# One threshold update for two query tiles in a bitwise search for the 256th largest score

## The chip, the cores and the metric

The kernel runs on one core of a Trainium2 chip. Its time is the device time of one execution, in microseconds (us); lower is better. Three runs of the kernel before took 3038.46, 3047.42 and 3047.6 us, so the median is 3047.42 us.

## The reference

Two transformer blocks run one after the other on a sequence of 1024 tokens with 1024 features. The change touches only the sparse attention of the first block. A small indexer scores every key for every query, and a query attends to its 256 best keys:

```python
dots = einsum('bthd,bsd->bths', qib, k_idx) * IDX_DIM ** -0.5      # 8 index heads, 64 wide
score = einsum('bth,bths->bts', wb * IDX_HEADS ** -0.5, relu(dots))
score = where(causal, score, -inf)
_, idx = top_k(score, 256)                                          # per query
...                                                                 # softmax over the 256 keys, 8 heads
```

The rest of the first block is a gated spatial unit, an output projection, and a feed-forward layer (FFN) of width 4096. The second block (a recurrence, a state space layer and another FFN) stands behind it and is not touched.

## The kernel before, in words

Tokens are cut into 8 query tiles of 128 rows, tile by tile on the 128 partitions. Tile `tt` can see keys up to its own end, so its scores are a matrix `sel[tt]` of 128 rows and (tt+1)*128 columns. Tiles 0 and 1 have at most 256 keys and need no search. The sequence is worked in two halves: tiles 0 to 3 (half A), beside the projections of both halves, and tiles 4 to 7 (half B), beside the output projection and the first FFN of half A.

The work on one tile has three steps. `index_score` (lines 622 to 649) makes the scores: TensorE products, a relu on ScalarE (L638), weighted sums on VectorE (L641, L643), and a causal fill on GpSimd (L648). `topk` (lines 651 to 698) finds, for each row, the value that 256 scores reach, one bit of its float pattern at a time. One bit is one step of three instructions on VectorE, each needing the one before: a count of the scores at or above the trial value (L669, over the whole row), a comparison of the count with 256 (L679, one element per partition) and the new trial value by bit operations (L680, one element per partition, two tensor inputs). There are 31 such steps per tile. Then the mask is written over the scores, ties included (L690 to L697). `attend` (lines 700 to 779) goes through the tiles in order, four pairs of heads each: TensorE products (L733, L734), mask and row maximum (L735), exponentials on ScalarE (L743), scaling (L746), transposes, a split in two parts (L760, L761), products with the values (L764), and sums into `ybT` (L770). The sums of squares of a finished tile (L778) feed `mix_in` (L803 to L818), which scales the attention result by L808 and L813 for the output projection `token_out`.

What sets the order of instructions on an engine is a scheduler with priorities and a model of times; each engine then runs its list in that order. The searches and everything marked `urgent` have the highest priority. Steps of two tiles whose code is in one call or in two are woven into one another wherever the scheduler finds both ready. Other projections and the FFN share VectorE with the searches: they empty TensorE's accumulators there (L302, L902) and split operands. GpSimd meanwhile makes the low parts of weights (L118) and sums for a modulation (L437).

In half A the calls are a search of tile 2 and one of tile 3. In half B they are one for tiles 4 and 5, one for 6, one for 7.

Of the kernel before, what the change touches and what calls it, by code (L numbers as in the profile page):

```python
# [8 lines left out]
F32 = mybir.dt.float32  # L9
F32R = mybir.dt.float32r  # L10
I32 = mybir.dt.int32
# [3 lines left out]
OP = mybir.AluOpType  # L15
# [6 lines left out]
HALF = 512  # L22
P = 128
# [11 lines left out]
class Kernel:  # L35
# [614 lines left out]

    def topk(self, tts):

        steps = [self.topk_steps(tt) for tt in tts if tt > 1]
        for _ in zip_longest(*steps):
            pass

    def topk_steps(self, tt):


        V = self.nc.vector  # L660
        n = (tt + 1) * P
        sel = self.sel[tt]
        junk = self.junk if tt > 3 else self.junk[:, tt % 2 * HALF:tt % 2 * HALF + HALF]

        def count(value, op):

            c = self.tinyS.tile([P, 4], I32, name=f"topk{tt % 2}")
            cnt = c[:, 0:1].bitcast(F32)
            V.tensor_scalar(junk[:, :n], sel, value, 0.0, op0=op, op1=OP.add, accum_out=cnt)  # L669
            return cnt, c[:, 1:2], c[:, 2:3]  # L670

        cnt, t, u = count(0.0, OP.is_ge)
        V.tensor_scalar(t, cnt, 256.0, 1.0, op0=OP.is_ge, op1=OP.subtract)
        V.tensor_scalar(u, t, 1 << 30, None, op0=OP.bitwise_xor)
        yield
        for b in range(30, -1, -1):
            t = u
            cnt, keep, u = count(t.bitcast(F32), OP.is_ge)
            V.tensor_scalar(keep, cnt, 256.0, float(1 << b), op0=OP.is_ge, op1=OP.mult)  # L679
            V.scalar_tensor_tensor(u, t, (1 << b) ^ (1 << b >> 1), keep, op0=OP.bitwise_xor, op1=OP.bitwise_xor)  # L680
            yield
        thr = u.bitcast(F32)
        before = count(thr, OP.is_gt)[0]
        ties = junk.bitcast(F16)
        k = ties.shape[1] // 2
        for c0 in range(0, n, k):
            w = min(k, n - c0)
            x = sel[:, c0:c0 + w]
            e, r = ties[:, :w], ties[:, k:k + w]
            V.tensor_scalar(e, x, thr, None, op0=OP.is_equal)  # L690
            V.tensor_tensor_scan(r, e, e, before, op0=OP.add, op1=OP.max)
            if c0 + w < n:
                before = self.tinyS.tile([P, 4], F32, name=f"topk{tt % 2}")[:, 0:1]
                V.tensor_copy(before, r[:, w - 1:w])
            V.scalar_tensor_tensor(r, r, 256.0, e, op0=OP.is_le, op1=OP.mult)
            V.scalar_tensor_tensor(x, x, thr, r, op0=OP.is_gt, op1=OP.add)
        V.tensor_scalar(sel, sel, -1.0, -MASKED, op0=OP.add, op1=OP.mult)  # L697
        yield

    def attend(self, tts, ybT, depth=1, through=True):  # L700

# [255 lines left out]
    def run(self):  # L957
        nc, I, tc = self.nc, self.I, self.tc
        with ExitStack() as at:
# [8 lines left out]
            with ExitStack() as sa:  # L968
                sg = self.pool("sgup", st=sa, side="right")
                self.ropep = self.pool("ropep", st=sa, side="right")  # L970
                self.score = self.pool("scoreA", st=sa, side="right")
                with ExitStack() as st:
                    tmp = self.pool("early", st=st)
                    self.cols_setup(tmp)
                    self.rope_setup(tmp)
                    self.cols_mod(tmp)
                    rows = [self.rowp.tile([P, D], F32, name="row") for j in range(3)]
                    rows.append(self.acc.tile([P, D], F32, name="acc"))
                    self.raws = self.pool("raws", 8, st=st)
                    sums = self.tp.tile([P, 512], F32, name="tp")  # L980

                    gains = lambda k0, k1: self.gain_part(k0, k1, sums)
                    biases = lambda k0, k1: self.ada_part(0, k0, k1, sums)
                    gains(0, PARTS[1])
                    rows = self.scaled_rows(rows, lambda t: I["x"][0, t * P:(t + 1) * P, :], scalar=True)
                    first = biases(0, PARTS[1])
                    next(first)
                    gen = self.norm_T(rows, self.s1, self.sh1, ("tp", "tp"), 3, PARTS[1:])
                    next(gen)
                    next(first, None)  # L990
                    hA = next(gen)

                    def parts():
                        for k0 in range(0, 8, 2):
                            if k0 and k0 in PARTS:
                                k1 = min([k for k in PARTS if k > k0] + [8])
                                gains(k0, k1)
                                for _ in biases(k0, k1):
                                    pass
                                next(gen)  # L1000
                            yield

                    self.wi = self.consts.tile([P, 8, 8], F32, name="wi")
                    self.sel = {}
                    self.ssx = {}
                    self.ssb = [self.consts.tile([P, 4], F32, name=f"ssb{i}") for i in range(2)]
                    self.proj(0, hA, "kvq", parts())
                    self.proj(0, hA, "qkw")

                    self.kT = self.k16.tile([P, 4, S], F32R, name="k16")  # L1010
                    self.kiT = self.kT[:, :, HALF:].rearrange("p (a b) t -> p a b t", a=2)
                    self.ki_stack(range(4))
                    for tt in (2, 3, 0, 1):
                        self.index_score(tt)
                self.ybp = long("ybp", 4)
                self.pT = long("pT", 2)
                self.proj(0, hA, "q")
                self.sgu_setup(sg)
                self.cols_rest()
                with ExitStack() as st:  # L1020
                    self.adac = self.pool("adac", 2, st=st)
                    self.pp = self.pool("ppA", 6, st=st)
                    self.vhl = [self.vp.tile([P, 4, 2, P], F32R, name="vhl0")]
                    p0 = tc.cur_priority
                    self.kv_stack(range(4))
                    ybA = [self.ybp.tile([P, HALF], F32, name="ybT") for k in range(4)]
                    with self.urgent():
                        self.topk((2,))
                        self.topk((3,))
                    with tc.high_priority(tc.cur_priority - p0):  # L1030
                        self.attend(range(4), ybA, 2)
                    self.proj(0, hA, "u")
                    rows = [self.rowp.tile([P, D], F32, name="row") for j in range(3)]
                    rows.append(self.adac.tile([P, D], F32, name="adac"))
                    rows = self.scaled_rows(rows, lambda t: I["x"][0, (4 + t) * P:(5 + t) * P, :])
                    hB = self.norm_T(rows, self.s1, self.sh1)
                    next(hB)
                    self.proj(0, hA, "v")
                    next(self.sgu_steps)
                    hB = next(hB)  # L1040
                    self.background = self.ada_rest()
                    for b in ("qkw", "kvq", "q", "u", "v"):
                        if b == "u":
                            mA = self.mix_gated(0)
                        self.proj(1, hB, b)
                        if b in ("qkw", "v"):
                            next(self.sgu_steps)
                    next(self.sgu_steps)
                    for _ in self.background:
                        pass  # L1050
                    self.ki_stack(range(4, 8))
                    G, mT = self.mix_in(0, mA, ybA)
            with ExitStack() as st:
# [14 lines left out]
                    self.kv_stack(range(4, 8))  # L1068
                ybB = [self.ybp.tile([P, HALF], F32, name="ybT") for k in range(4)]
                with self.urgent():  # L1070
                    for tts in ((4, 5), (6,), (7,)):
                        self.topk(tts)
                with tc.high_priority(tc.cur_priority - p0):
                    self.attend(range(4, 8), ybB)
# [796 lines left out]
```

## Time and profile before

| what | value |
|---|---|
| median of 3 runs | 3047.42 us |
| profiled execution | 3063.16 us, of which the span is 3061.4 us |
| TensorE busy (matmul) | 2831.0 us, 92% of the span |
| VectorE busy | 1745.7 us, 57% |
| ScalarE busy | 1245.3 us, 41% |
| GpSimd busy | 1460.9 us, 48% |
| mean granted TensorE clock | 0.96 |
| 192 counts (L669) with a trial value | 179.5 us of VectorE |

The profiled execution lasted a little longer than the three runs. TensorE's share is a mean over stages: in the slices of the span between about 150 and 310 us it is busy seven tenths, while VectorE is busy nine tenths or more. VectorE is also that full from about 460 to 840 us, where TensorE is full too.

### The profile page before, as it was taken

The numbers are of one execution on the slowest core, as the hardware profiler recorded it, in microseconds if no ns is written. First come the engines' busy times: TensorE is split into PE (matmuls) and PEld (weight loads), VectorE is DVE, ScalarE is ACT, GpSimd is POOL, SyncE is SP. The second block draws the span as 40 slices with busy tenths as digits, with TensorE's granted clock in tenths as the row PEclk, the third lists the DMA queues.
The fourth block names the chain that finished last, engine by engine and source line by source line (L and its number), as shares of the span: only waits on it lengthen the run. The fifth ranks groups of instructions, "written<-read, shape, count | busy, mean of one in ns | idle before, by whom it ended". The sixth has DMA issues, their size and how long they took to land.

```text
span 3061.4 us, 42378 instructions
## 1 busy us (share of the span) xinstructions
PE 2831.0 (92%) x15600; PEld 2337.1 (76%) x15600; DVE 1745.7 (57%) x3752; ACT 1245.3 (41%) x2121; POOL 1460.9 (48%) x1285
## 2 busy tenths in 40 slices
PE   6977998999998899889989999998899999999998
PEld 5865776787887777667777888887777778888887
DVE  5699569999946944445563563433655634332122
ACT  4545555444455333343333443332433333433333
POOL 4665544544445743434433465443343435454444
PEclk9988999999999999899999999999999999999999
DMA  7445332222224555333225484653323235442232
GB/s 252 136 130 178 124 118 64 90 79 69 73 84 148 179 164 152 103 86 90 76 84 147 147 274 123 178 147 107 81 92 90 82 90 155 141 131 97 97 97 83
DMA packets 301504, 370.22 MB, mean 121 GB/s; under 512 B 70936, under 2 KB 209902, under 8 KB 301040
## 3 DMA queue, kind: packets, MB, share of 16 engines
q1 hardware_dynamic: 293296, 351.75, 37.9%
q10 hardware_dynamic: 8000, 15.76, 1.5%
q8 instruction: 123, 2.02, 0.3%
q14 instruction: 85, 0.70, 0.1%
HBM read 315.80 MB, written 51.65 MB: 120 GB/s over the span
## 4 chain that ended last, share of the span: by engine, by line
PE 57%; DVE 27%; DMA 8%; issue 3%; ACT 2%; SPq 2%; POOL 1%; ACTq 0%; POOLq 0%; DVEq 0%
PE mm L66 16%; PE mm L68 16%; PE mm L69 16%; DVE junk L669 4%; DMA L<-lt_d 3%; DVE T L1389 2%; DVE Ttmp L1387 2%; DVE topk L680 2%; PE tp L128 1%; DVE acc L902 1%; DVE score L643 1%; DVE p L746 1%; DMA TT<-tt_d 1%; DVE p L735 1%; PE tp L764 1%
## 5 line engine op out<-in xcount | busy, mean ns | idle before, releaser
L118 POOL TENSOR_TENSOR whl<-wraw,whl 128x512 fp32r<-128x512 f32 (+1 forms) x836 | 1134.7, 1382 | 1255.7 <-ACT whl L116 1187.1
L66 PE MATMUL mm<-hT,whl 128*128 128x512 f32 x1760 | 699.1, 398 | 21.6 <-DVE acc L902 13.5
L68 PE MATMUL mm<-hT,whl 128*128 128x512 f32 x1760 | 701.6, 400 | 0.0
L69 PE MATMUL mm<-hT,whl 128*128 128x512 f32 x1760 | 694.8, 397 | 3.9 <-POOL whl L118 3.9
L116 ACT CAST whl<-wraw 128x1024 fp32r<-128x1024 f32 (+1 forms) x418 | 435.1, 1042 | 541.5 <-PE mm L69 389.7
L66 PE MATMUL mm<-whl,hT 128*128 128x512 f32 (+1 forms) x1584 | 614.6, 402 | 42.9 <-DVE acc L902 18.5
L68 PE MATMUL mm<-whl,hT 128*128 128x512 f32 (+1 forms) x1584 | 625.6, 396 | 0.4 <-POOL whl L118 0.4
L69 PE MATMUL mm<-whl,hT 128*128 128x512 f32 (+1 forms) x1584 | 614.3, 396 | 0.9 <-DVE hT L61 0.9
L66 PEld LDWEIGHTS mm<-hT,whl 128*128 128x128 f32 x1760 | 336.1, 191 | 97.2 <-DVE acc L902 15.2
L69 PEld LDWEIGHTS mm<-hT,whl 128*128 128x128 f32 x1760 | 336.3, 191 | 73.7 <-POOL whl L118 5.0
L66 PEld LDWEIGHTS mm<-whl,hT 128*128 128x128 f32 x1584 | 305.2, 193 | 112.2 <-DVE acc L902 22.2
L68 PEld LDWEIGHTS mm<-hT,whl 128*128 128x128 f32 x1760 | 336.1, 191 | 66.3 <-issue 0.9
L68 PEld LDWEIGHTS mm<-whl,hT 128*128 128x128 f32 x1584 | 305.9, 193 | 60.7 <-issue 1.2
L69 PEld LDWEIGHTS mm<-whl,hT 128*128 128x128 f32 x1584 | 303.3, 192 | 62.2 <-DVE hT L61 1.8
L902 DVE TENSOR_TENSOR acc<-mm,acc 128x512 f32<-128x512 f32 x240 | 160.6, 686 | 189.2 <-PE mm L69 188.7
L61 DVE TENSOR_TENSOR hT<-sm,hT 128x512 fp32r<-128x512 f32 x112 | 94.4, 846 | 265.2 <-ACT hT L60 264.5
L881 ACT ACTIVATE sm<-mm 128x512 f32<-128x512 f32 x128 | 76.5, 598 | 273.1 <-PE mm L69 267.3
L669 DVE TENSOR_SCALAR_CACHE_REDUCE junk<-score,topk 128x640 uint8<-128x640 f32 (+4 forms) x192 | 179.5, 941 | 1.8
L1387 DVE TENSOR_TENSOR Ttmp<-L,T 128x60 f32<-128x60 f32 (+24 forms) x248 | 77.8, 314 | 95.5 <-DMA L<-lt_d 88.1
L60 ACT CAST hT<-sm 128x512 fp32r<-128x512 f32 x144 | 89.3, 620 | 31.0 <-DVE sm L1835 28.3
L764 PE MATMUL tp<-pT,vhl 128*128 128x256 f32 x288 | 64.1, 310 | 25.0 <-ACT pT L760 7.4
L743 ACT ACTIVATE p<-p,nm 128x128 f32<-128x128 f32 (+7 forms) x64 | 49.6, 778 | 91.4 <-DVE nm L739 60.5
(470 smaller groups left out, 3489.2 us busy)
## 6 DMA issues: line engine op xcount, KB each, us to landing
wraw<-w_ff SPq DMA_DIRECT2D x128, 512.0 KB
wraw<-w_in SPq DMA_DIRECT2D x100, 512.0 KB
wraw<-w_ff_up SPq DMA_DIRECT2D x64, 512.0 KB
wraw<-w_ff_down SPq DMA_DIRECT2D x64, 512.0 KB
wraw<-w_ada SPq DMA_DIRECT2D x32, 512.0 KB
wraw<-w_out SPq DMA_DIRECT2D x32, 512.0 KB
raw<-w_ada SPq DMA_DIRECT2D x16, 512.0 KB
x_d<-acc ACTq DMA_DIRECT2D x16, 512.0 KB
```

The lines of the kernel that those rows point to most:

```text
L60: self.nc.scalar.copy(hi, src)
L61: (engine or self.nc.gpsimd).tensor_tensor(lo, src, hi.bitcast(F32), op=OP.subtract)
L66: nc.tensor.matmul(ps, a[0], b[0], start=start, stop=False)
L68: nc.tensor.matmul(ps, a[0], b[1], start=False, stop=False)
L69: nc.tensor.matmul(ps, a[1], b[0], start=False, stop=stop)
L116: nc.scalar.copy(hl[:, 0], raw)
L118: nc.gpsimd.tensor_tensor(hl[:, 1, s], raw[:, s], hl[:, 0, s].bitcast(F32), op=OP.subtract)
L669: V.tensor_scalar(junk[:, :n], sel, value, 0.0, op0=op, op1=OP.add, accum_out=cnt)
L764: nc.tensor.matmul(o, self.vhl[(s0 + i) // 4][:, (s0 + i) % 4, kv, :], t[:, x, 256 * i:256 * i + 256], start=(s0 + i + x == 0), stop=(s0 + ...
L881: nc.scalar.activation(r, ps, AF.Relu)
L902: nc.vector.tensor_tensor(d, pss[j], d, op=OP.add)
L1387: V.tensor_tensor(tmp[:, :n, :w], L[:, j:j + 1, j + 1:].to_broadcast([P, n, w]), T[:, :n, j:j + 1].to_broadcast([P, n, w]), op=OP.mult)
```

## The change

`topk` no longer makes one generator per tile. It counts for every tile of its argument, and puts the counts side by side in one small tile, so that the comparison and the new trial value are done by one instruction each for all the tiles of a call, on one or two elements per partition. After the last bit the masks are written tile by tile as before, by the new function `mark`. Half A now calls the search once for tiles 2 and 3, half B once for 4 and 5 and once for 6 and 7.

```diff
     def topk(self, tts):
-        steps = [self.topk_steps(tt) for tt in tts if tt > 1]
-        for _ in zip_longest(*steps):
-            pass
+        V = self.nc.vector
+        tts = [tt for tt in tts if tt > 1]
+        m = len(tts)
+        def counts(values, op):
+            c = self.tinyS.tile([P, 4, 2], I32, name="topk")
+            cnt = c[:, 0, :m].bitcast(F32)
+            for i, tt in enumerate(tts):
+                V.tensor_scalar(junk(tt)[:, :(tt + 1) * P], self.sel[tt], values[i], 0.0, op0=op, op1=OP.add,
+                                accum_out=cnt[:, i:i + 1])
+            return cnt, c[:, 1, :m], c[:, 2, :m]
...
+        for b in range(30, -1, -1):
+            t = u
+            cnt, keep, u = counts(floats(t), OP.is_ge)
+            V.tensor_scalar(keep, cnt, 256.0, float(1 << b), op0=OP.is_ge, op1=OP.mult)
+            V.scalar_tensor_tensor(u, t, (1 << b) ^ (1 << b >> 1), keep, op0=OP.bitwise_xor, op1=OP.bitwise_xor)
+        before = counts(floats(u), OP.is_gt)[0]
+        for i, tt in enumerate(tts):
+            self.mark(tt, junk(tt), u[:, i:i + 1].bitcast(F32), before[:, i:i + 1])
...
-                        self.topk((2,))
-                        self.topk((3,))
+                        self.topk((2, 3))
...
-                    for tts in ((4, 5), (6,), (7,)):
+                    for tts in ((4, 5), (6, 7)):
                         self.topk(tts)
```

In the new code the count is L667, the comparison L680 and the new trial value L681; lines of `attend` and `mix_in` are 6 higher than before (L764 is L770, L778 is L784, L808 is L814).

On VectorE, one bit of tiles 2 and 3 where both were under way reads like this before (`topk0` and `topk1` are the small tiles of the even and the odd query tile, `score2` and `score3` the scores of tiles 2 and 3):

```order
L669 TENSOR_SCALAR junk_188,topk0_1340<-score2_855,topk0_1336 128x384
L669 TENSOR_SCALAR junk_188,topk1_1443<-score3_928,topk1_1439 128x512
L679 TENSOR_SCALAR topk0_1340<-topk0_1340 128x1
L679 TENSOR_SCALAR topk1_1443<-topk1_1443 128x1
L680 SCALAR_TENSOR_TENSOR topk0_1340<-topk0_1336,topk0_1340 128x1
L680 SCALAR_TENSOR_TENSOR topk1_1443<-topk1_1439,topk1_1443 128x1
```

And this is the start of the common search in the changed kernel, its first bit and the next one's counts:

```order
L667 TENSOR_SCALAR junk_188,topk_1297<-score2_855,topk_1292 128x384
L667 TENSOR_SCALAR junk_188,topk_1297<-score3_928,topk_1292 128x512
L680 TENSOR_SCALAR topk_1297<-topk_1297 128x2
L681 SCALAR_TENSOR_TENSOR topk_1297<-topk_1292,topk_1297 128x2
L667 TENSOR_SCALAR junk_188,topk_1302<-score2_855,topk_1297 128x384
L667 TENSOR_SCALAR junk_188,topk_1302<-score3_928,topk_1297 128x512
```

The four small instructions of a bit became two, each on two elements per partition, and each now needs the one before it.

A little earlier on VectorE, while the scores of tile 3 were being summed, the list before had steps of tile 2 between those sums:

```order
L641 TENSOR_SCALAR score3_928<-smS_953,wi_394 128x512
L669 TENSOR_SCALAR junk_188,topk0_1324<-score2_855,topk0_1320 128x384
L643 SCALAR_TENSOR_TENSOR score3_928<-smS_959,wi_394,score3_928 128x512
L679 TENSOR_SCALAR topk0_1324<-topk0_1324 128x1
L300 TENSOR_TENSOR hT_2642<-sm_2648,hT_2642 128x512
L643 SCALAR_TENSOR_TENSOR score3_928<-smS_965,wi_394,score3_928 128x512
L680 SCALAR_TENSOR_TENSOR topk0_1324<-topk0_1320,topk0_1324 128x1
```

In the changed kernel only the sums and the projections' own work stand there:

```order
L641 TENSOR_SCALAR score3_928<-smS_953,wi_394 128x512
L643 SCALAR_TENSOR_TENSOR score3_928<-smS_959,wi_394,score3_928 128x512
L643 SCALAR_TENSOR_TENSOR score3_928<-smS_965,wi_394,score3_928 128x512
L300 TENSOR_TENSOR hT_2545<-sm_2551,hT_2545 128x512
L643 SCALAR_TENSOR_TENSOR score3_928<-smS_971,wi_394,score3_928 128x512
L302 TENSOR_SCALAR sm_2581<-mm_2576,cola_263 128x512
```

Every step of tile 2 moved behind the last sum of tile 3.

The third place is on TensorE, at the end of the first FFN, where the second output projection waits for the attention of tiles 4 to 7. Before, the rows just ahead of `mix_in` (L808) were matmuls of that projection:

```order
L66 MATMUL mm_9709<-whl_9742,hT_7379 128x512
L68 MATMUL mm_9709<-whl_9742,hT_7379 128x512
L69 MATMUL mm_9709<-whl_9742,hT_7379 128x512
L66 MATMUL mm_9709<-whl_9742,hT_7387 128x512
L68 MATMUL mm_9709<-whl_9742,hT_7387 128x512
L69 MATMUL mm_9709<-whl_9742,hT_7387 128x512
L808 MATMUL tp_9510<-ident_94,rs_9508 128x128 x4
```

In the changed kernel the rows ahead of it (L814) belong to the attention of tile 7, with its products with the values (L770) and transposes of its weights (`p`):

```order
L770 MATMUL tp<-pT,vhl_1223 128x256
L128 MATMUL tp<-ident,p 128x128 x4
L770 MATMUL tp<-pT,vhl_1223 128x256 x3
L128 MATMUL tp<-ident,p 128x128 x8
L770 MATMUL tp<-pT,vhl_1223 128x256 x4
L770 MATMUL tp<-pT,vhl_4033 128x256 x8
L784 MATMUL tp<-ones,smS 128x1 x4
L814 MATMUL tp<-ident,rs 128x128 x4
```

In all, 39 products (L770), 32 transposes and four pairs of score products of tile 7 moved behind the last matmul that the projection can do without the attention; from L814 on TensorE's list is the same in both kernels.

## Rows read from the trace of the kernel before

**Rows 1.** Busy time by stretch: length, PE, PEld, DVE, ACT, POOL, granted clock, DMA
```profile
120.00:320.00 200.00, 157.68 (x791) 132.85 (x790) 196.81 (x582) 107.44 (x216) 127.00 (x113) 0.88 0.47 149
480.00:620.00 140.00, 128.39 (x575) 104.39 (x574) 139.05 (x364) 67.20 (x120) 68.14 (x62) 0.98 0.25 78
640.00:940.00 300.00, 295.84 (x1508) 249.96 (x1508) 239.87 (x581) 141.25 (x242) 132.85 (x102) 0.99 0.24 76
```

**Rows 2.** TensorE's longest wait between 140 and 340: total us, times, longest
```profile
PE mm L66 <- ACT sm L298: 9.4, 1, 9.4
```

**Rows 3.** One bit of tile 2 alone: start, us, instruction
```profile
122.21 0.61 DVE L669 TENSOR_SCALAR_CACHE_REDUCE junk<-score,topk 128x384 uint8<-128x384 f32 x1
122.75 0.08 DVE L669 DVE_READ_ACCUMULATOR junk<-score,topk 128x1 f32 x1
122.87 0.15 DVE L679 TENSOR_SCALAR topk<-topk 128x1 int32<-128x1 f32 x1
123.06 0.16 DVE L680 SCALAR_TENSOR_TENSOR topk<-topk,topk 128x1 int32<-128x1 int32 x1
123.25 0.61 DVE L669 TENSOR_SCALAR_CACHE_REDUCE junk<-score,topk 128x384 uint8<-128x384 f32 x1
```

**Rows 4.** One bit of tiles 2 and 3 woven, after both counts
```profile
166.96 0.27 DVE L679 TENSOR_SCALAR topk<-topk 128x1 int32<-128x1 f32 x2
167.14 0.28 DVE L680 SCALAR_TENSOR_TENSOR topk<-topk,topk 128x1 int32<-128x1 int32 x2
167.33 0.61 DVE L669 TENSOR_SCALAR_CACHE_REDUCE junk<-score,topk 128x384 uint8<-128x384 f32 x1
```

**Rows 5.** VectorE and GpSimd around a late new trial value
```profile
153.03 1.74 POOL L118 TENSOR_TENSOR whl<-wraw,whl 128x328 fp32r<-128x328 f32 x2
154.16 2.99 DVE L680 SCALAR_TENSOR_TENSOR topk<-topk,topk 128x1 int32<-128x1 int32 x2
154.73 2.40 POOL L437 TENSOR_TENSOR adac<-adac,wraw 128x1024 f32<-128x1024 f32 x1
157.07 0.60 DVE L669 TENSOR_SCALAR_CACHE_REDUCE junk<-score,topk 128x384 uint8<-128x384 f32 x1
```

**Rows 6.** Three lines' instructions: ns min/median/max, first and last start us
```profile
L680 DVE SCALAR_TENSOR_TENSOR topk<-topk,topk x186: 144/159/4205, 123.1 to 810.6; 128x1 int32<-128x1 int32 x186
L679 DVE TENSOR_SCALAR topk<-topk x186: 129/145/156, 122.9 to 810.0; 128x1 int32<-128x1 f32 x186
L690 DVE TENSOR_SCALAR junk<-score,topk x21: 270/344/1464, 246.7 to 830.2; 128x256 f16<-128x256 f32 x12, 128x128 f16<-128x128 f32 x9
```

**Rows 7.** L680 by stretch: length, VectorE busy us, granted clock, DMA
```profile
118.00:146.00 28.00, 2.28 (x10) 1.00 0.32 97
146.00:245.00 99.00, 21.39 (x41) 0.83 0.48 152
245.00:320.00 75.00, 6.72 (x12) 0.90 0.51 160
430.00:615.00 185.00, 21.48 (x62) 0.95 0.28 87
```

**Rows 8.** Last score product of tile 3, and its causal fill
```profile
139.08 0.39 PE L636 MATMUL tp<-k,qT 128*128 128x512 f32 x1
145.34 0.29 POOL L648 TENSOR_SCALAR_AFFINE_SELECT score<-score 128x128 f32<-128x128 f32 x1 [2.33 <-DVE score L643]
```

**Rows 9.** From the attention's last products to the projection that needs it
```profile
951.85 0.52 PE L764 MATMUL tp<-pT,vhl 128*128 128x256 f32 x3
962.80 0.39 PE L69 MATMUL mm<-whl,hT 128*128 128x512 f32 x1
968.51 2.08 PE L808 MATMUL tp<-ident,rs 128*128 128x128 f32 x8 [5.33 <-POOL rs L78]
975.43 0.79 PE L66 MATMUL mm<-whl,hT 128*128 128x512 f32 x1 [3.05 <-ACT hT L815]
```

**Rows 10.** Busy time in the ten microseconds around that projection's restart
```profile
970.00:980.00 10.00, 6.70 (x21) 4.93 (x21) 9.86 (x15) 3.22 (x6) 9.71 (x15) 0.50 0.74 254
```

More of the change, by code (lines that the diff above doesn't have):

```diff
@@ L651, in topk, with junk, floats, mark @@
     def topk(self, tts):
-        steps = [self.topk_steps(tt) for tt in tts if tt > 1]
-        for _ in zip_longest(*steps):
-            pass
-    def topk_steps(self, tt):
+        V = self.nc.vector
+        tts = [tt for tt in tts if tt > 1]
+        m = len(tts)
+        def junk(tt):
+            return self.junk if tt > 3 else self.junk[:, tt % 2 * HALF:tt % 2 * HALF + HALF]
+        def counts(values, op):
[5 more added lines that the diff above has]
+            return cnt, c[:, 1, :m], c[:, 2, :m]
+        def floats(t):
+            return [t[:, i:i + 1].bitcast(F32) for i in range(m)]
+        cnt, t, u = counts([0.0] * m, OP.is_ge)
+        V.tensor_scalar(t, cnt, 256.0, 1.0, op0=OP.is_ge, op1=OP.subtract)
+        V.tensor_scalar(u, t, 1 << 30, None, op0=OP.bitwise_xor)
+        for b in range(30, -1, -1):
[6 more added lines that the diff above has]
+            self.mark(tt, junk(tt), u[:, i:i + 1].bitcast(F32), before[:, i:i + 1])
+    def mark(self, tt, junk, thr, before):
         V = self.nc.vector
@@ L662, in topk_steps @@
         sel = self.sel[tt]
[L663 to L683, printed above, removed]
         ties = junk.bitcast(F16)
@@ L692, in topk_steps @@
             if c0 + w < n:
-                before = self.tinyS.tile([P, 4], F32, name=f"topk{tt % 2}")[:, 0:1]
+                before = self.tinyS.tile([P, 4, 2], F32, name="topk")[:, 0, 0:1]
                 V.tensor_copy(before, r[:, w - 1:w])
@@ L697, in topk_steps @@
         V.tensor_scalar(sel, sel, -1.0, -MASKED, op0=OP.add, op1=OP.mult)
-        yield
     def attend(self, tts, ybT, depth=1, through=True):
```

## The prediction

> **What bounds the kernel now.** I read the busy times by stretch first, since the shares of the whole span hide where the searches stand. From 120 to 320 us, where tiles 2 and 3 are searched, VectorE is busy 196.81 of 200 us and TensorE 157.68, with a granted clock of 0.88 of full speed: half A waits for VectorE [rows 1]. The reader is to see TensorE's longest wait there, 9.4 us for an accumulator that ScalarE L298 empties [rows 2]; ScalarE and VectorE take turns at emptying, and VectorE's list was full of search steps. From 480 to 620 us (tiles 4 and 5) VectorE is full again, 139.05 of 140, while TensorE idles 11.6 us. From 640 to 940 us, where tiles 6 and 7 are searched and attended, TensorE is busy 295.84 of 300 us, so a faster search has nothing to give there [rows 1]. So what counts is VectorE's work up to 320 us, a little of it up to 620 us, and how the attention of tile 7 meets the end of the FFN.
>
> **The change part by part.** The counts stay as they are, 32 per tile and one for ties. VectorE's list is 202 rows shorter, so the change does what it says; TensorE's list behind the first FFN is unaltered.
>
> *Small instructions, unblocked.* One bit of a tile alone takes 123.25 - 122.21 = 1.04 us, of which 0.50 us pass from the reading of the count (122.75) to the next count [rows 3]. Two woven tiles take only 167.33 - 166.96 = 0.37 us for all four small instructions, because each stands behind one that it does not need [rows 4]. In the changed list each needs its predecessor, and I price the new pair at the 0.50 us of the single chain (at best 0.37 us, where other work stands between). In half A ten steps of tile 2 ran alone before 146 us [rows 7], and about as many of tile 3 alone at the end, so about 20 bits were woven: before, 20 x 0.37 + 22 x 0.50 = 18.4 us; after, 31 x 0.50 = 15.5 us. That saves 3 us, not half.
>
> *The blocked update.* L680 takes 0.16 us when free [rows 3], but up to 4.2 us in all [rows 6]. The reader is to see why in one place: L680 starts at 154.16, while GpSimd's L118 runs, gets through, and the second one sits until 157.07, just after GpSimd's L437 (154.73 + 2.40 = 157.13 by a rough record) [rows 5]. In half A the 63 records of L680 sum to 2.28 + 21.39 + 6.72 = 30.4 us, so 63 x 0.16 = 10.1 us is work and 20.3 us is waiting [rows 7]. For tiles 4 and 5 it is 21.48 - 62 x 0.16 = 11.6 us. Halving the number of L680 would halve that, if nothing else became blockable. But the comparison widens from one element to two. One element wide, L679 was never held: its longest of 186 took 156 ns. The same kind of instruction 128 or 256 wide, L690, was: from 270 to 1464 ns [rows 6]. Two wide is not in the trace. If it behaves like the narrow row, half A saves 20.3 / 2 = 10 us more; if like the wide row, a bit of two tiles has two instructions that can be held, as now, and nothing is saved. I take the second: the pair now runs back to back as the two L680 did in rows 5, so GpSimd's next instruction can slip between them.
>
> [...]
>
> *The late start.* Tile 2 did ten steps, 10 x 1.04 = 10.4 us, while tile 3's scores were being made. The changed list has nothing in their place, so VectorE idles there. It gets part back: tile 3's last score product is done by 139.5, but its fill came at 145.3, after 2.33 us of GpSimd waiting for VectorE's sums [rows 8]. Without the steps between them I put that at 142, so 3.4 us return and 7 us are lost (5 to 10.4).
>
> *Half A together.* 7 - 3 = +4 us on VectorE, of which I count +3 in the time, since VectorE is not full after 320 us. Bounds: +10.4 with no step saved and no earlier fill, and -9 if the waits halve as well and only 4 us are lost.
>
> *Tiles 4 and 5* were woven already, with other work in the gaps: 0, or down to -6 if the waits halve, of which -3 reach TensorE's 11.6 us of idle time. *Tiles 6 and 7*: VectorE saves something, TensorE is full, so 0. What hides it is the FFN's matmuls.
>
> *The end of the FFN.* Tile 6 now gets its mask together with tile 7, so its attention comes later, and 39 products, 32 transposes and 8 score products of tile 7 stand behind the last projection matmul that needs no attention. The products ran three in 0.52 us [rows 9]; at 0.17 us also for the transposes and 0.39 us for the score products it is 6.8 + 5.4 + 3.1 = 15 us of TensorE's work. It is moved, not added: the matmuls ahead of it end 15 us sooner. What is added is idle time. Before, the way from the last product (952.4) to the first matmul that uses it (975.4) took 23 us, and projection matmuls covered it until 963.2, leaving 5.33 + 3.05 = 8.4 us of idle time [rows 9]. Now nothing covers it. Bare, it takes between the 6.9 us from L808 on and the old 23 us; much of the 23 was waiting behind other work, so I take 12 us. The end costs 12 - 8.4 = +4 us (-2 to +15), plus what the attention itself makes TensorE wait (0 to 5).
>
> The sum is 3 + 0 + 0 + 4 = +7 us on the profiled 3063.16 us, a ratio of 1.0023. On the median of 3047.42 us that is 3054 us.
>
> **The rivals.** (a) is the forecast: the two-wide comparison can be held. For it speaks the wide row in rows 6; against it, that two elements are far closer to one.
>
> (b) It can't be held, and the waits halve. Half A is then 7 - 3 - 10 = -6 us, tiles 4 and 5 -3, the end +4: -5 us, so 3042 us. For it speaks that 186 narrow ones never waited.
>
> [...]
>
> **How the numbers follow.** What a measurement of this kernel can tell from no change is about 0.3%, here 9 us. I give (a) 0.47, (b) 0.35, (c) 0.18. Within (a), from -6 to +18 us, a third lies above +9 and almost nothing below -9; within (b), from -16 to +6, four in ten lie below -9; (c) is slower in nine of ten. Faster: 0.35 x 0.42 + 0.02 = 0.17. Slower: 0.47 x 0.34 + 0.18 x 0.9 = 0.32. Same: 0.51. The range runs from 3034 us (the better half of (b)) to 3074 us (into (c)); of (a) alone it would be 3042 to 3066 us.
>
> **What would show it.** For (a): records of L680 (the new comparison) of over 0.5 us, dozens of them, and waits of L680 and L681 together about the old 20 us in half A; for (b) none over 0.2 us and L681 at half the old wait. The late start shows as 5 us or more of VectorE idle between the first count of tile 2 and that of tile 3. The end shows as the time from the last matmul before L814 to the first behind it, and the granted clock there. I am wrong altogether if TensorE's idle time between 140 and 320 us falls by 15 us or more: then VectorE's other work, which now stands earlier in its list than the search, was worth more than the search itself.

## The result: 0.6 to 0.9 per cent slower

The changed kernel took 3075.02 us in the median of 7 runs, the kernel before 3047.42 us; the ratio is 1.009 (95% interval 1.0068 to 1.0113; it leaves out one disturbed run of 3565 us). A second measurement on another chip gave 3069.58 against 3047.59 us, 1.0064 [1.0046, 1.0082]. The forecast was 3054 us, within 3034 to 3074 us. So the change costs 20 to 27 us where I had +7, and it costs most of them in other places than I had named.

The two profiled executions hide this: that of the changed kernel (3064.63 us) was its fastest run, that of before (3063.16 us) was 16 us above its median. TensorE's first matmuls of one line of the second block, and the same line's in that block's later part, show it: before, then after.

```profile
1204.59 1.16 PE L1371 MATMUL tp<-zw,wgu 128*128 128x128 f32 x8
2426.24 1.16 PE L1371 MATMUL tp<-zw,wgu 128*128 128x128 f32 x8
```
```profile
1218.24 1.16 PE L1376 MATMUL tp<-zw,wgu 128*128 128x128 f32 x8
2430.03 1.16 PE L1376 MATMUL tp<-zw,wgu 128*128 128x128 f32 x8
```

The changed kernel is 13.7 us late when the first block is done; before's execution then lost 9.9 us in code that both share. What the change did has to be read in the first 1100 us.

**After, by stretch** (length, PE, PEld, DVE, ACT, POOL, granted clock, DMA), to set against [rows 1]:

```profile
120.00:140.00 20.00, 20.00 (x102) 16.70 (x102) 12.01 (x16) 14.82 (x22) 11.44 (x9) 1.00 0.33 98
120.00:320.00 200.00, 160.28 (x787) 135.21 (x787) 182.19 (x508) 107.63 (x211) 131.28 (x116) 0.88 0.50 156
640.00:940.00 300.00, 284.11 (x1421) 239.44 (x1420) 231.80 (x505) 131.82 (x226) 130.00 (x100) 0.98 0.24 76
780.00:820.00 40.00, 31.93 (x139) 25.99 (x139) 38.69 (x75) 13.18 (x20) 17.07 (x13) 0.87 0.28 86
940.00:1020.00 80.00, 70.96 (x367) 58.41 (x366) 66.50 (x192) 44.96 (x89) 39.63 (x62) 0.96 0.41 129
```

Three of these stretches of the kernel before:

```profile
120.00:140.00 20.00, 20.00 (x103) 16.77 (x102) 18.60 (x49) 13.69 (x20) 10.27 (x8) 1.00 0.34 100
780.00:820.00 40.00, 40.00 (x207) 34.26 (x206) 39.20 (x95) 19.62 (x37) 19.45 (x15) 1.00 0.25 79
940.00:1020.00 80.00, 70.14 (x334) 57.36 (x333) 61.73 (x182) 39.10 (x80) 47.47 (x74) 0.91 0.56 172
```

The reader is to see three things. VectorE lost 6.6 us of work between 120 and 140: the late start. TensorE, "full" from 640 to 940 before, now idles 15.9 of 300 us, half of it between 780 and 820. And from 940 to 1020, where I had put +4 us, nothing got worse: TensorE idles 9.0 us against 9.9.

**The two small instructions after** (ns min/median/max, first and last start), to set against [rows 6]; L680 is now the comparison, L681 the new trial value:

```profile
L680 DVE TENSOR_SCALAR topk<-topk x93: 145/169/2385, 148.3 to 785.8; 128x2 int32<-128x2 f32 x93
L681 DVE SCALAR_TENSOR_TENSOR topk<-topk x93: 139/160/2358, 148.5 to 786.0; 128x2 int32<-128x2 int32 x93
```

One element wide, 186 comparisons took 156 ns at most [rows 6]; two wide, 32 of 93 took more than 500 ns, and the longest 2385 ns. Who holds them stands in the changed kernel's timeline (start, us, instruction), VectorE and GpSimd around two of them:

```profile
497.61 1.64 POOL L61 TENSOR_TENSOR hT<-sm,hT 128x512 fp32r<-128x512 f32 x1 [3.25 <-ACT hT L60]
498.01 1.26 DVE L680 TENSOR_SCALAR topk<-topk 128x2 int32<-128x2 f32 x1
502.86 1.56 POOL L61 TENSOR_TENSOR hT<-sm,hT 128x512 fp32r<-128x512 f32 x1
503.19 1.26 DVE L680 TENSOR_SCALAR topk<-topk 128x2 int32<-128x2 f32 x1
```

The first pair ends at 499.25 and 499.27, the second at 504.42 and 504.45: here the comparison sits until GpSimd's instruction is done (GpSimd's spans are rough, so the match is good to what they can show). The busy time of L680, then of L681, by stretch:

```profile
142.00:245.00 103.00, 11.02 (x21) 0.90 0.51 158
245.00:320.00 75.00, 6.55 (x11) 0.82 0.54 166
430.00:615.00 185.00, 14.14 (x31) 0.94 0.26 84
...
142.00:245.00 103.00, 10.46 (x20) 0.90 0.51 158
245.00:320.00 75.00, 6.18 (x11) 0.82 0.54 166
430.00:615.00 185.00, 12.81 (x31) 0.94 0.26 84
```

Half A: 34.2 us in 63 records, less 63 x 0.16 of work: 24 us of waiting, where there were 20.3 [rows 7]. Tiles 4 and 5: 26.95 - 62 x 0.16 = 17 us, where there were 11.6. The same code's waits differ from kernel to kernel: by this sum, the old lines waited 14 to 21 us in half A and 10 to 13 at tiles 4 and 5 in the seven kernels (that before among them) that leave those tiles to them. Both new numbers lie above. As many instructions as before can be held, and they wait longer, not equally long.

**Around tile 6's mask**, TensorE and then VectorE of the changed kernel:

```profile
805.59 1.12 PE L128 MATMUL tp<-ident,p 128*128 128x128 f32 x4 [4.76 <-DVE mx L741]
810.01 0.80 PE L66 MATMUL mm<-whl,hT 128*128 128x512 f32 x1 [3.31 <-DVE acc L908]
811.03 0.63 PE L69 MATMUL mm<-whl,hT 128*128 128x512 f32 x1
```
```profile
803.73 0.62 DVE L704 TENSOR_SCALAR score<-score 128x896 f32<-128x896 f32 x1
804.92 0.60 DVE L741 CUSTOM_DVE_ANT_0 p<-tp,score 128x448 f32<-128x448 f32 x1
809.29 1.26 DVE L908 TENSOR_TENSOR acc<-mm,acc 128x512 f32<-128x512 f32 x2
822.02 0.69 DVE L704 TENSOR_SCALAR score<-score 128x1024 f32<-128x1024 f32 x1
```

The mask of tile 6 is finished (L704) at 804.3; until then TensorE's next instruction, transposes of tile 6's exponentials, can't go, and the FFN's matmuls stand behind it. Then the FFN waits 3.3 us for an accumulator (L908), since VectorE first masks tile 6's products (L741) and works on tile 7's mask, which lasts until 822.7. After the gap the same matmul takes 0.63 us instead of 0.39 [rows 9]: from 804 to 812, with TensorE idle for most of the time, its granted clock is 0.50, where it was 1.00 before.

```profile
804.00:812.00 8.00, 3.10 (x9) 2.34 (x10) 7.93 (x25) 3.58 (x6) 1.44 (x2) 0.50 0.15 51
```

Before, tile 6 had its mask by 721, 113 us before tile 7.

**Around tile 2's mask** the same happens in half A. The mask of tile 2 (L704, 384 wide) in the changed kernel, TensorE's transposes that wait for it, then the mask in the kernel before (L697):

```profile
292.49 0.35 DVE L704 TENSOR_SCALAR score<-score 128x384 f32<-128x384 f32 x1
293.83 1.11 PE L128 MATMUL tp<-ident,p 128*128 128x128 f32 x4 [7.44 <-DVE mx L741]
```
```profile
263.51 2.13 DVE L697 TENSOR_SCALAR score<-score 128x384 f32<-128x384 f32 x1
```

Tile 2's mask is ready 27 us later than before, since it now waits for the last bit of tile 3 too, and TensorE idles 7.4 us in one gap ahead of it.

### The profile page after: what moved, and what is told of

The parts are those of the page before. It is cut to its first block, busy times and chain, and to the rows that moved or that the text cites. A ratio compares the mean times of both kernels' runs of the same rounds, so it can differ in the third digit from the quotient of the medians.

```text
span 3062.9 us, 42174 instructions
## 1 busy us (share of the span) xinstructions
PE 2831.0 (92%) x15600; PEld 2337.3 (76%) x15600; DVE 1735.1 (57%) x3560; ACT 1249.9 (41%) x2123; POOL 1455.7 (48%) x1285
## 4 chain that ended last, share of the span: by engine, by line
PE 49%; DVE 24%; DMA 7%; issue 2%; SPq 1%; ACT 1%; POOL 1%; ACTq 0%; POOLq 0%; DVEq 0%
PE mm L69 14%; PE mm L66 14%; PE mm L68 14%; DVE junk L667 4%; DMA L<-lt_d 3%; DVE Ttmp L1392 3%; DVE T L1394 3%; DVE acc L908 1%; DVE score L643 1%; PE tp L128 1%; DVE topk L681 1%; DVE topk L680 1%; DMA TT<-tt_d 1%; DVE p L741 1%; DMA tt_d<-T 1%
## 5 line engine op out<-in xcount | busy, mean ns | idle before, releaser
L908 DVE TENSOR_TENSOR acc<-mm,acc 128x512 f32<-128x512 f32 x240 | 160.4, 685 | 193.8 <-PE mm L69 193.3
L667 DVE TENSOR_SCALAR_CACHE_REDUCE junk<-score,topk 128x384 uint8<-128x384 f32 (+2 forms) x192 | 178.5, 942 | 3.7
L1394 DVE TENSOR_TENSOR T<-T,Ttmp 128x60 f32<-128x60 f32 (+24 forms) x248 | 77.7, 313 | 7.7
L888 ACT ACTIVATE sm<-sm 128x512 f32<-128x512 f32 x128 | 80.7, 630 | 2.0
```

The lines of the kernel that those rows point to most:

```text
L667: V.tensor_scalar(junk(tt)[:, :(tt + 1) * P], self.sel[tt], values[i], 0.0, op0=op, op1=OP.add, accum_out=cnt[:, i:i + 1])
L888: nc.scalar.activation(r, r, AF.Square)
L908: nc.vector.tensor_tensor(d, pss[j], d, op=OP.add)
L1394: V.tensor_tensor(T[:, :n, j + 1:], T[:, :n, j + 1:], tmp[:, :n, :w], op=OP.subtract)
```

## The experiments

Ratios are against the kernel before on the same chip, with 95% intervals. 0.001 is 3 us. The scheduler plans the whole list anew for every kernel, so other work shifts a little with each edit too.

**One pair at a time.** Three kernels search one of the pairs by the changed code and leave the others to the old one (the edits are against the changed kernel):

```diff
 pairA_only
-                    for tts in ((4, 5), (6, 7)):
-                        self.topk(tts)
+                    for tts in ((4, 5), (6,), (7,)):
+                        self.topk_one(tts)
 pair45_only
-                        self.topk((2, 3))
+                        self.topk_one((2,))
+                        self.topk_one((3,))
-                    for tts in ((4, 5), (6, 7)):
-                        self.topk(tts)
+                    self.topk((4, 5))
+                    self.topk_one((6,))
+                    self.topk_one((7,))
```

(topk_one is the old function; pair67_only has the calls for tiles 2 and 3 as in pair45_only, then topk_one((4, 5)) and topk((6, 7)).)

> Only tiles 2 and 3 are searched together; 4 and 5, 6, 7 as before. Mask theory: 3 to 7 us faster than before or equal (ratio 0.997 to 1.0), mix_in of half A starts about 6 us earlier. Held-update theory and late-start theory: 3 to 10 us slower (1.001 to 1.003).

> Only tiles 4 and 5 share an update; the rest as before. Mask theory: no change within 0.2%. Held-update theory: the masks of tiles 4 and 5 come 5 to 15 us later than before and the kernel is 0.2 to 0.4% slower.

> Only tiles 6 and 7 are searched together; the rest as before. Mask theory: all of the loss or more, ratio 1.007 to 1.012, with a gap of TensorE of 7 us or more just ahead of the mask of tile 6 and mix_in 12 us or more later than before. Held-update theory: a third of the loss, about 1.003.

Measured: tiles 2 and 3 alone 1.0022 [1.0011, 1.0034], 4 and 5 alone 1.0044 [1.0027, 1.0060], 6 and 7 alone 1.0047 [1.0029, 1.0066]. Each pair costs. My first theory, that the two masks of tiles 6 and 7 back to back are the cause, wanted 1.007 or more there and nothing at tiles 4 and 5, which cost as much. The changed kernel again, on the same chip:

> The changed kernel once more, as the measure for the three that pair one search alone. Mask theory (TensorE starves while it waits for the joint mask of tiles 6 and 7, and the attention's tail stands bare behind the FFN): 0.7 to 1.1% slower than before, TensorE idle 7 us or more in one gap near 800 us. Held-update theory (the widened comparison can be held by GpSimd, so VectorE loses more than it saves in every search): the same total, but spread over all three searches.

It gave the 1.0064 above, less than the sum of the three, 1.0113.

**Taking the sharing back, in all pairs.** First the comparison alone, then the new trial value too, then a new trial value of another kind:

```diff
 narrow_cmp, unshared, pairs_scalar
-            V.tensor_scalar(keep, cnt, 256.0, float(1 << b), op0=OP.is_ge, op1=OP.mult)
+            for i in range(m):
+                V.tensor_scalar(keep[:, i:i + 1], cnt[:, i:i + 1], 256.0, float(1 << b), ...)
 unshared also
+            for i in range(m):
+                V.scalar_tensor_tensor(u[:, i:i + 1], t[:, i:i + 1], ..., keep[:, i:i + 1], ...)
 scalar_upd (in the kernel before; pairs_scalar the same, per tile)
-            V.scalar_tensor_tensor(u, t, (1 << b) ^ (1 << b >> 1), keep, op0=OP.bitwise_xor, ...)
+            V.tensor_scalar(u, t, (1 << b) ^ (1 << b >> 1), keep, op0=OP.bitwise_xor, ...)
```

> The changed kernel, with the comparison L680 done once per tile on one element per partition, as before the change; the new trial value stays shared. Theory 1 (the two-wide comparison is held by GpSimd, and that ate the saving): in the changed kernel the 31 comparisons of a pair take 0.42 us of VectorE each for tiles 4 and 5 and 0.53 for tiles 2 and 3, against 0.07 and 0.09 for each of the 62 before, so 8 us come back in the one and 11 us in the other, less where another instruction is held in its place: 1.000 to 1.004 times the time before. Theory 2 (the order of the pairs costs the time: late start, two masks back to back, tile 7's attention in the tail): no change against the changed kernel, 1.006 to 1.009.

Measured: 1.0015 [1.0005, 1.0026]. Theory 1 holds. The comparison of narrow_cmp, one element wide again, and its shared new trial value:

```profile
L681 DVE TENSOR_SCALAR topk<-topk x186: 132/148/155, 147.8 to 784.3; 128x1 int32<-128x1 f32 x186
...
L682 DVE SCALAR_TENSOR_TENSOR topk<-topk x93: 145/240/2310, 148.1 to 784.5; 128x2 int32<-128x2 int32 x93
```

In the same pairs and order, none of 186 is held.

> The changed kernel with nothing shared in a bit: comparison and new trial value are done per tile, one element wide, in the changed kernel's order (both counts, both comparisons, both new values), for the same pairs. Theory 1 (sharing made a second instruction that GpSimd holds): the comparisons are free again, the 62 updates of a pair wait about as long as the 62 before; only the order of the pairs of tiles 6 and 7 is left of the cost, 1.000 to 1.005 times the time before. Theory 2 (the order costs the time): 1.006 to 1.009, as the changed kernel.

Measured: 1.0074 [1.0057, 1.0091], which theory 1 did not allow: the order alone costs 22 us. So both theories hold a part: the order costs 0.7%, the shared update earns 0.6%, and the shared comparison gives 0.5 to 0.7% away again.

> The kernel before, in its order, where the new trial value is one TENSOR_SCALAR with the kept bit as its scalar operand, in place of the instruction with two tensor inputs. Theory 1 (the update is held because it has two tensor inputs; one element wide with one input, like the old comparison, it is not): the waits of about 20 us in half A and 12 us at tiles 4 and 5 go, of which half or more reach the end: 0.990 to 0.997 times the time before. Rival (GpSimd gets its turn from VectorE in any case, so the wait goes to the next instruction that can be held): 0.998 to 1.002, with the emptying or split instructions longer by as much.

Measured: 3025.76 us, 0.9914 [0.9900, 0.9928]. This version beats both kernels, by 25 us and by some 45 to 55. Its new trial value:

```profile
L680 DVE TENSOR_SCALAR topk<-topk,topk x186: 193/208/217, 124.5 to 800.0; 128x1 int32<-128x1 int32 x186
```

Its busy time between 140 and 320 us, and that of the kernel before:

```profile
140.00:320.00 180.00, 146.63 (x723) 123.36 (x722) 171.26 (x542) 99.22 (x201) 127.97 (x112) 0.86 0.54 168
```
```profile
140.00:320.00 180.00, 137.68 (x690) 116.08 (x689) 178.21 (x534) 93.75 (x196) 116.73 (x105) 0.87 0.49 154
```

It is 0.05 us longer in the median (0.208 against 0.159) and is never held: 217 ns at most, where the two-input form reached 4205 [rows 6]. TensorE works 9 us more in the stretch. The rival falls with the time. But a part of the waits did move on: VectorE's busy time there fell by 7 us only, where 20 us of waiting went and the slower form added 3. The largest group that waits longer, in the kernel before and in scalar_upd (line, shapes, count, then busy us and mean ns):

```profile
L538 DVE CUSTOM_DVE_ANT_0 sm<-acc 128x128 f32<-128x128 f32 x16 | 4.4, 330 | 0.0
```
```profile
L538 DVE CUSTOM_DVE_ANT_0 sm<-acc 128x128 f32<-128x128 f32 x16 | 11.0, 740 | 0.0
```

> As unshared, with the update as a TENSOR_SCALAR with the kept bit as scalar operand, per tile: the changed kernel's order with nothing in a bit that GpSimd is expected to hold. Theory 1: 0.992 to 1.000 times the time before, a few us slower than the kernel before with the same update, by the order of tiles 6 and 7. Theory 2 (order): at least 1.004.

Measured: 0.9963 [0.9949, 0.9977]. No comparison or update of a bit is held here, and against the 0.9914 of the old order with the same update the changed order still costs 0.5%, 15 us. So neither theory covers it alone.

**Where the order costs.** Tiles 6 and 7 in one call or two, and pairs alone with nothing shared:

```diff
 narrow_split67 (of narrow_cmp), scalar_split67 (of pairs_scalar)
-                    for tts in ((4, 5), (6, 7)):
+                    for tts in ((4, 5), (6,), (7,)):
 unshared67, unsharedA, unshared45: pair67_only, pairA_only, pair45_only with unshared's two loops
 narrow67, narrowA, narrow45: the same three with narrow_cmp's loop
```

> The changed kernel with the comparison done per tile, one element wide, and with tiles 6 and 7 searched in two calls, one after the other, as before. Theory 1 (what is left of the cost in the kernel with the narrow comparison, 1.0015, is the order at tiles 6 and 7: both masks back to back while TensorE waits for tile 6's, 7 to 8 us of TensorE's idle time between 780 and 860 us): TensorE is busy 78 us or more of 780 to 860 again, and the time is 0.996 to 0.999 of that before. Theory 2 (what is left is the late start in half A): 1.001 to 1.003, as before this edit.

> The kernel with the changed order and nothing in a bit that GpSimd holds (0.9963), with tiles 6 and 7 searched one after the other again; tiles 2 and 3, and 4 and 5, stay in pairs. Theory 1 (the order costs at tiles 6 and 7 alone): as the kernel before with the same update, 0.990 to 0.993. Theory 2 (the late start in half A costs the difference): 0.995 to 0.997. In between, both cost.

> The kernel before with tiles 6 and 7 alone searched as a pair, in the changed order, but with comparison and update done per tile, one element wide. Theory 1 (the order at tiles 6 and 7): 1.003 to 1.006, no better than the same pair with shared instructions, 1.0047, and TensorE busy 74 us or less of 780 to 860. Theory 2 (the pair cost because its comparison is held): 0.999 to 1.002.

Measured: 1.0004 [0.9991, 1.0017], 0.9963 [0.9949, 0.9977] and 1.0018 [1.0008, 1.0028]. Splitting 6 and 7 gives 0.1% back in the one kernel, which the noise covers, and nothing in the other. My theory that the order costs mainly at tiles 6 and 7 fell: 1.0018 is all that it costs there, and the rest of the pair's 1.0047 comes with what it shares.

> The kernel before with only tiles 2 and 3 searched as a pair, in the changed order, but with comparison and update done per tile, one element wide. Theory 1 (the order costs mainly by the late start in half A): 1.003 to 1.006. Theory 2 (the order costs at tiles 4 and 5, where two bits now run in step): 0.999 to 1.002. The prediction's own price for the late start, +4 us less no saving, is 1.001.

> The kernel before with only tiles 4 and 5 searched in the changed order (both counts, both comparisons, both updates), nothing shared. Theory 1 (late start in half A): no change, 0.999 to 1.002, since these two tiles were woven before. Theory 2 (two bits in step expose what a bit of the other tile used to hide): 1.003 to 1.005.

> The kernel before with only tiles 2 and 3 as a pair, the update shared and the comparison per tile, one element wide. If the shared update halves the waits and nothing is held in its place, 0.996 to 0.999, by the prediction's case (b) for half A alone (6 us less). If the halved waits go to the next instruction that GpSimd can hold, as the pair with both shared, 1.001 to 1.003.

> The kernel before with only tiles 4 and 5 in the changed order, the update shared and the comparison per tile, one element wide. Theory 1 (the held comparison costs): 0.997 to 1.000, against 1.0044 with both shared. Theory 2 (two bits in step cost): still 1.002 to 1.004.

> The kernel before with only tiles 6 and 7 as a pair, the update shared and the comparison per tile, one element wide. Nothing shared it was 1.0018, both shared 1.0047. If the held comparison made the difference, as at tiles 4 and 5 (1.0009 against 1.0044): 1.000 to 1.003. If the shared update did, the pair being in step: 1.004 to 1.006.

| pair | order alone | + shared update | + shared comparison |
|---|---|---|---|
| 2, 3 | 1.0040 [1.0027, 1.0054] | 1.0017 [1.0004, 1.0030] | 1.0022 [1.0011, 1.0034] |
| 4, 5 | 1.0000 [0.9987, 1.0013] | 1.0009 [0.9995, 1.0024] | 1.0044 [1.0027, 1.0060] |
| 6, 7 | 1.0018 [1.0008, 1.0028] | 0.9992 [0.9977, 1.0006] | 1.0047 [1.0029, 1.0066] |
| all | 1.0074 [1.0057, 1.0091] | 1.0015 [1.0005, 1.0026] | 1.0064 [1.0046, 1.0082] |

The first theories of unsharedA and unshared45 hold. narrowA lies in its second range, but against unsharedA the shared update earned 7 us there (1 to 13); narrow45 and narrow67 lie between or just beside their ranges, nearer to the held comparison as the cause.

The order costs in half A, 12 us (8 to 16), and a little at tiles 6 and 7; two bits in step, at tiles 4 and 5, cost nothing that can be told from zero. The shared comparison costs nothing that can be told in half A (the 24 us of waiting there are little more than unsharedA's 32.90 - 62 x 0.16 = 23), and 11 us (4 to 17) and 17 us (10 to 24) at the other two pairs.

Two causes are open for the 12 us of half A, and no run takes them apart: VectorE's late start, and tile 2's mask, which comes only with tile 3's. That the late start alone costs them is not shown.

In unsharedA VectorE is busy 11.48 us from 120 to 140, 7 us less than before, and tile 3's mask ends 13 us later than in the kernel before, so the late start is about half of that delay. Tile 2's mask ends at 302.3 there, 37 us later than before, and TensorE waits 4.5 us for it. The stretch and tile 3's mask in unsharedA, then before's mask:

```profile
120.00:140.00 20.00, 20.00 (x102) 16.71 (x101) 11.48 (x16) 14.76 (x23) 11.20 (x9) 1.00 0.31 96
```
```profile
315.34 1.51 DVE L706 TENSOR_SCALAR score<-score 128x512 f32<-128x512 f32 x1
```
```profile
303.41 0.43 DVE L697 TENSOR_SCALAR score<-score 128x512 f32<-128x512 f32 x1
```

At tiles 4 and 5, tile 5's mask (ready at 618.7 in the kernel before) in unshared45, narrow45 and pair45_only:

```profile
612.43 0.56 DVE L706 TENSOR_SCALAR score<-score 128x768 f32<-128x768 f32 x1
```
```profile
621.17 1.54 DVE L705 TENSOR_SCALAR score<-score 128x768 f32<-128x768 f32 x1
```
```profile
628.07 1.53 DVE L704 TENSOR_SCALAR score<-score 128x768 f32<-128x768 f32 x1
```

And busy times from 430 to 615: of narrow45's shared update, of narrow_cmp's, then of pair45_only's comparison and update.

```profile
430.00:615.00 185.00, 18.43 (x31) 0.94 0.26 83
```
```profile
430.00:615.00 185.00, 15.29 (x31) 0.94 0.27 87
```
```profile
430.00:615.00 185.00, 13.25 (x31) 0.93 0.27 86
430.00:615.00 185.00, 15.04 (x31) 0.93 0.27 86
```

Half as many updates wait 18.43 - 31 x 0.16 = 13.5 us in narrow45, but 6 of them are one record, and 15.29 - 31 x 0.16 = 10.3 us in narrow_cmp (10.1 in narrow_split67): little or no less than the 62 before (11.6, [rows 7]). With the comparison held as well it is 28.29 - 62 x 0.16 = 18.4 us (17 in the changed kernel, 20 in its second profile). VectorE is nearly full there (from 480 to 620 us busy 139.05 of 140 us before [rows 1], 134.60 in the changed kernel), the mask comes later by 7 us than in narrow45, and the time is longer by 11. A later mask is not the price by itself, though: narrow45's comes 10 us after unshared45's, for 3 us of time that the noise covers.

The one long record of narrow45, and what GpSimd did meanwhile:

```profile
556.58 6.20 DVE L682 SCALAR_TENSOR_TENSOR topk<-topk 128x2 int32<-128x2 int32 x1
```
```profile
556.44 5.08 POOL L118 TENSOR_TENSOR whl<-wraw,whl 128x512 fp32r<-128x512 f32 x4
561.44 1.32 POOL L61 TENSOR_TENSOR hT<-sm,hT 128x512 fp32r<-128x512 f32 x1
```

The update sat through five instructions of GpSimd in a row, not through one.

At tiles 6 and 7 TensorE between 780 and 820 us, in pair67_only and in unshared67:

```profile
780.00:820.00 40.00, 31.98 (x148) 26.19 (x147) 36.17 (x70) 16.13 (x30) 20.32 (x15) 0.96 0.25 78
```
```profile
780.00:820.00 40.00, 36.73 (x174) 30.11 (x172) 34.63 (x69) 16.72 (x31) 17.46 (x14) 0.96 0.24 75
```

The gap at tile 6's mask is 3.3 us deep by the order and 8.0 with both instructions shared. That goes with 5 us of the 9 between these two. It was 5.6 us in narrow67, which is not slower than the kernel before, so the gap alone does not set the time; where the rest of the 17 us between narrow67 and pair67_only goes is open.

## Why the prediction was wrong, step by step

*Small instructions and the late start.* The price of a bit was right: where nothing was held or stood between, it was 0.52 us in the changed kernel (148.17 to 148.69, for one), against my 0.50; the 3 us that I drew from it were not measured by themselves. The late start was there too: VectorE idled 8.0 us from 120 to 140, as said, against 1.4. But tile 3's first count of the changed kernel, with its one wait, stands at

```profile
144.05 0.69 DVE L667 TENSOR_SCALAR_CACHE_REDUCE junk<-score 128x512 uint8<-128x512 f32 x1 [0.40 <-POOL score L648]
```

Before, the fill ended at 145.63 [rows 8]. So 1.6 us came back, not the 3.4 that I had counted. The 6.6 us that VectorE lost from 120 to 140 are near my 7, but the order as a whole costs 12 us in half A (unsharedA): I had left out that tile 2's mask now waits for tile 3's search. Half A came out at +7 us (pairA_only, 3 to 10) against my +3: the right sign, inside my bounds, and in part by luck, since the shared update, which I had put at nothing, earned 7 back.

*The blocked update.* Case (a) was right that the two-wide comparison is held (dozens of records over 0.5 us were its sign, and 32 came), and (b) fell. Where the rows of 128 or 256 elements (1464 ns at most) and that of a single element (156 ns) were the bounds [rows 6], two elements went with the wide ones: 2385 ns at most. Why they do is not shown.

What I drew from (a), that as many holdable instructions wait as long as before, is **the step that failed**, and with it *Tiles 4 and 5: 0*, which was in truth +13 us (pair45_only), 11 of them by the held comparison. As many were held, 18 of 62 over 0.3 us before and 20 in pair45_only, but each for longer, about 0.6 us beyond its own 0.16 before and 0.9 now. So the waits rose from 11.6 to between 17 and 20 us, while sharing the update alone left them at 10 to 13.5. Why each hold is longer was not followed further.

*Tiles 6 and 7: TensorE is full, so 0* is the second step that failed, by +14 us (pair67_only). TensorE was full (40.00 of 40 us from 780 to 820) because tile 6's mask came 83 us earlier than now. I moved that mask in my own account only as far as the tail, and did not ask what TensorE, which takes its list in order, would meet at 800 us: its next instruction waiting for a mask, with FFN matmuls ready behind it.

*The end of the FFN, +4 us*, did not come: TensorE's idle time from 940 to 1020 is about the same. The attention of tile 7 itself made TensorE wait 2.9 us (L739, for L741), inside my 0 to 5; the wait ahead of the scaling shrank and that behind it all but vanished [rows 9]:

```profile
PE tp L814 <- POOL rs L78: 2.4, 1, 2.4
PE mm L66 <- ACT hT L821: 0.7, 1, 0.7
```

So (c), that this end decides, at 0.18 and slower in nine of ten, had the right direction for another cause. No run shows the loss at the end of the FFN that its part in the chances and the 3074 us at the top of the range stand for: from 940 to 1020 TensorE's granted clock is 0.96 after and 0.91 before, with 9.0 us idle against 9.9.

The sum was 3 + 0 + 0 + 4; measured alone, the parts are 7, 13 and 14, with the end in the last of them. They add up to 34 us; together they took 27 us in the first measurement, which agrees with the sum within the noise, and 20 in the second, which does not. Whether they overlap is open.

## What to carry to other kernels

Merging two tiny instructions into one two elements wide was a loss at tiles 4 to 7 here, where 19 of 62 wide comparisons took more than 0.5 us (1300 ns at most) and the narrow one 156 ns at most: look at the longest record of each form, not the median, which was 169 against 145 ns over all pairs. What helped was to give the held instruction a form that was not held (217 ns at most against 4205), even though it is 0.05 us slower in the median; the kernel with it took 0.9914 of the time before (scalar_upd). And before calling an engine full, ask what in its list now comes due later: TensorE was busy 40.00 of 40 us from 780 to 820 before and 31.93 after, with 4.76 us in one gap ahead of transposes that waited for tile 6's mask and FFN matmuls behind them in its list.

## What was not expected of the hardware

- A `TENSOR_SCALAR` on one element per partition, with its second operand as a per-partition scalar, was not held in scalar_upd: 193 to 217 ns in 186 records, against 144 to 4205 ns of the `SCALAR_TENSOR_TENSOR` that does the same with two tensor inputs.
- The time that GpSimd holds VectorE did not follow the number of instructions that can be held: at tiles 4 and 5, 62 updates waited 11.6 us, 31 shared ones 10.1 to 13.5 in three kernels, and 31 with 31 shared comparisons 17 to 20.
- A hold can outlast one instruction of GpSimd: an update sat 6.20 us through five of them in narrow45, and the longest of the kernel before, 4205 ns, spans three.
